# ScalarE issues the mixers' own transfers in a two-layer hybrid backbone block

## The chip, the cores and the metric

The kernel runs on one core of a Trainium2 chip. The metric is the device time in microseconds (us) of one execution. A core has five engines with an instruction stream each: PE (TensorE, matmuls), DVE (VectorE), ACT (ScalarE), POOL (GpSimd) and SP (SyncE, which only issues transfers). Each stream is executed in order: an instruction that waits for a semaphore holds up all that follow it on its engine.

## The reference

Two layers of one trunk work on 512 latent tokens and a prefix of 256 context tokens, 1024 channels each, all in float32:

```
for layer in range(2):
    p_lat, p_ctx = (modulated rmsnorm of x, of ctx) @ w_in          # 1024 -> 256 + 1560 + 1536 columns
    y = concat(s5_mixer, gdn_mixer, rwkv_mixer)                     # three groups of heads
    x = x + gt1 * (y_lat @ w_out)
    x = x + gt2 * (square(relu(h @ w1)) @ w2)                       # h: modulated rmsnorm, 1024 -> 4096 -> 1024
    if layer == 0: the same for ctx with y_ctx
return rmsnorm(x)
```

The S5 mixer is a complex diagonal scan in both directions. The gated DeltaNet (GDN) and RWKV-7 mixers have 6 heads of 64 channels each. Both are delta rules: in chunks of 64 tokens they need the inverse of a unit triangular 64x64 matrix per chunk, head and direction, and then a scan over the chunks, from both ends. The latents' scans start from the state that the context's scans leave.

## The kernel before

Activations lie with channels on the 128 partitions and tokens in the free dimension, 256 for the context and 512 for the latents.

**Dense work.** The projections, the modulations and the MLP stream their weights from DRAM. `weight` (L265) loads a tile of 128x512 into one of four staging tiles `wl` (L271, issued by SP), ACT casts it to the rounded format in one of three `wh` (L272), and POOL or DVE subtracts to get the rest in one of two `wo` (L273). `product` (L290) then runs three matmuls per weight and activation tile (L296) into the PSUM bank `d`. The modulations (`mods`, L921) load float32 weights (L934) and multiply them as they are (L937).

**Mixers.** `run_jobs` goes through 12 pairs of jobs, one GDN and one RWKV job of two heads each: three pairs for each of context and latents in both layers. For a pair come, in this order, `prep` of both jobs, `solve`, `prep2`, `post` of both (after `level2`, which joins the inverses of 32x32 blocks to those of 64x64), `chain` and `readout`. `solve` (L335) brings the blocks through DRAM into a layout with a problem in each partition (L352, L363, L364), inverts them on DVE (L368 to L373) and takes them back (L376 to L386), all with transfers issued by SP. ACT copies a half of the matrices in it (L366, L375).

A job moves its own data by these lines, all of which SP issues before the change:
- `source` (L1319) loads a projection that `front` stored to DRAM (L1028): keys, queries, values, decays and gates, in `prep` and `readout`.
- `park` (L1326) stores a tile to a DRAM scratch until it is wanted: GDN's queries and attention matrices, RWKV's bonus, its read matrices `R` and its transposed `kb`.
- `fetch` (L1332) loads a parked tile back in `post` or `readout`.
- In `GdnJob.post`, L1469 loads halves of the parked attention matrices beside the scaled queries, which ACT copies in L1470.

Of the code that reads or writes what they carry: ACT's L1562 squares a key that `source` loaded; POOL's L1465 scales the queries that `fetch` loaded; ACT's L1656 evicts what `prep2` parks; PE's L481 transposes.

**Memory and order.** Tiles of the mixers and activations are pieces of 18 pages in SBUF (`s`, L184). A piece that is taken again waits until its last readers are done. The order of the instructions on each engine is written when the kernel is built, by the scheduler of the tile framework: it takes the instructions with priorities (`prio`, L117; classes L33, chains first, dense work late), runs them through its own estimate of times, and puts each into the stream of its engine when its operands are there by that estimate. The hooks of `run` (L1252) say behind which pair the dense stages are traced.

Of the kernel before, what the change touches and what calls it, by code (L numbers as in the profile page):

```python
# [89 lines left out]
class Kern:  # L90
# [132 lines left out]
    def wide(self, tag, dt=F32):  # L223
        return self.wp.tile([P, 512], dt, tag=tag, name=self.nm(tag), bufs={"wl": 4, "wh": 3, "wo": 2}[tag])
# [259 lines left out]
    def by_head(self, p, nt, flip, keep):  # L484

        nc = self.nc
        o = self.s(nt * 128, keep=keep).rearrange("p (c v) -> p c v", v=64)
        for h in range(2):
            for r, rs in enumerate(HALVES):
                nc.scalar.copy(o[HALVES[1 - h if flip else h], r::2], p[rs].rearrange("p (t h v) -> p t h v", t=nt, h=2)[:, :, h])  # L490
        return o
# [814 lines left out]
class Job:  # L1306
# [9 lines left out]
    def source(self, j, keep=None):  # L1316
        K = self.K
        t = K.s(self.part.n, keep=keep)
        K.nc.sync.dma_start(t, K.pd[self.l, self.part][j])  # L1319
        return t  # L1320

    def park(self, name, t):

        w = t.shape[-1]
        dram = self.K.scratch(f"{name}{w}", [P, w], 3)
        self.K.nc.sync.dma_start(dram, t)  # L1326
        return dram

    def fetch(self, dram, keep):
        w = dram.shape[-1]  # L1330
        t = self.K.s(w, keep=keep)
        self.K.nc.sync.dma_start(t, dram)  # L1332
        return t

    def gather(self, ot, po, n):
# [11 lines left out]
class GdnJob(Job):  # L1347
# [82 lines left out]
    def post(self):  # L1430

        K, f, part, nt = self.K, self.f, self.part, self.nt
        nc, gd, n, C = K.nc, K.gd[self.l, part], part.n, part.nc
        K.level2(lambda h: nt, self.ytt, C, "q")
        wide = lambda keep: K.s(128 * C, keep=keep).rearrange("p (n d v) -> p n d v", d=2, v=64)
        ne = wide(None)
        nc.vector.tensor_tensor(ne, nt, gd["neg"][:, :, f].rearrange("p d c -> p c d").unsqueeze(3).to_broadcast([P, C, 2, 64]), OP.mult)
        self.W, self.TV = wide(self.till_chain), wide(self.till_chain)
        for n0 in range(0, C, 4):
            for w in range(2):  # L1440
                ps = K.ps("q").rearrange("p (n d v) -> p n d v", d=2, v=64)
                for i in range(4):
                    for d in range(1 if w else 2):
                        c = part.chunk(d, n0 + i)
                        for h, hs in enumerate(HALVES):
                            if w:
                                nc.tensor.matmul(ps[HALVES[1 - h], i], self.ku[hs, c], ne[hs, c], start=True, stop=True)
                            else:
                                nc.tensor.matmul(ps[hs, i, d], nt[hs, c, d], self.vh[hs, c], start=True, stop=True)
                nc.scalar.copy((self.W if w else self.TV)[:, n0:n0 + 4], ps)  # L1450


        self.kh, self.out = [], []
        for d in range(2):
            x = K.s(n, keep=self.till_chain).rearrange("p (c k) -> p c k", c=C)
            nc.gpsimd.tensor_tensor(x, self.ku, gd["bk"][:, d, f].unsqueeze(2).to_broadcast([P, C, 64]), OP.mult)
            self.kh.append(x)
        if self.emit:
            q_tm = self.fetch(self.q_tm, None)
        for d in range(2 if self.emit else 0):  # L1460
            x = K.s(2 * n, keep=self.till_chain).rearrange("p (h t) -> p h t", h=2)
            with K.scope():
                qd = K.s(n)
                by_head = lambda z: z.rearrange("p (t h k) -> p t h k", t=part.nt, h=2)
                nc.gpsimd.tensor_tensor(by_head(qd)[:, :, ::-1], by_head(q_tm),  # L1465
                                        gd["eg"][:, d, :, 2 * f:2 * f + 2].unsqueeze(3).to_broadcast([P, part.nt, 2, 64]), OP.mult)
                ps = K.transposed(qd, part.nt, "q")
                for h, hs in enumerate(HALVES):
                    nc.sync.dma_start(x[hs, h], self.at[hs, d * n:(d + 1) * n])  # L1469
                    nc.scalar.copy(x[HALVES[1 - h], h], ps[HALVES[1 - h]])  # L1470
            self.out.append(x)
        K.release(self.till_post)
# [68 lines left out]
class RwkvJob(Job):  # L1541
# [121 lines left out]
    def post(self):  # L1663
# [6 lines left out]
        for n0 in range(0, part.nc, 4):  # L1670
            with K.scope():
# [19 lines left out]
                for h, hs in enumerate(HALVES):  # L1691
                    nc.scalar.copy(xv[h][hs, nn], ps[hs])
        fetch = lambda t, p: self.fetch(t, self.till_chain).rearrange(p, i=64, n=part.nc)
        self.kb = [fetch(t, "p (n h i) -> p n h i") for t in self.kb]
        self.R = [fetch(t, "p (h n i) -> p h n i") for t in self.R]
        K.release(self.till_post)

# [230 lines left out]
```

## Time and profile before

| | |
|---|---|
| median of 3 runs | 3006.74 us (2999.44 to 3011.88) |
| profiled execution | 2999.21 us, of which the span of the trace is 2997.4 us |
| granted TensorE clock, mean | 0.883 of full speed |
| busy: PE, DVE, ACT, POOL | 2656.7, 1583.8, 1204.1, 1049.6 us |
| transfers | 401.65 MB, the 16 DMA engines 42.9% busy with those of the program |

The page gives busy times, the span in slices, the costliest groups of instructions and the issues of transfers. Engines are named as above, PEld is the loading of weights into PE, SPq is SP's stream. A row such as `ACT wh L272 <- PE d L296: 406.1, 238, 6.7` says that ACT, before the instructions of line 272 that write `wh`, waited 406.1 us in total, 238 times, 6.7 us at the longest, and that the wait ended when PE finished an instruction of line 296. In the timelines the bracket at a row's end gives the engine's idle time before the instruction and what ended it; "issue" means that the profile shows nothing that did. Issuing a transfer does not count as busy time.

### The profile page before, as it was taken

The numbers are of one execution on the slowest core, as the hardware profiler recorded it, in microseconds if no ns is written. First come the engines' busy times: TensorE is split into PE (matmuls) and PEld (weight loads), VectorE is DVE, ScalarE is ACT, GpSimd is POOL, SyncE is SP. The second block draws the span as 40 slices with busy tenths as digits, with TensorE's granted clock in tenths as the row PEclk, the third lists the DMA queues.
The fourth block names the chain that finished last, engine by engine and source line by source line (L and its number), as shares of the span: only waits on it lengthen the run. The fifth ranks groups of instructions, "written<-read, shape, count | busy, mean of one in ns | idle before, by whom it ended". The sixth has DMA issues, their size and how long they took to land. (4 is left out here: it accounts for less than half of the span.)

```text
span 2997.4 us, 54389 instructions
## 1 busy us (share of the span) xinstructions
PE 2656.7 (89%) x20052; PEld 2042.6 (68%) x20052; DVE 1583.8 (53%) x4047; ACT 1204.1 (40%) x2460; POOL 1049.6 (35%) x1227
## 2 busy tenths in 40 slices
PE   5889998876899999987989989889888989799998
PEld 2767875654668888866667777667655566478776
DVE  7744874764557756557765531547656353321213
ACT  3344443232435444455433434454333332243333
POOL 1432333423132221222447434343433323144443
PEclk9889997676899999977999999889987868699999
DMA  5445545544764544443343332365465622023222
GB/s 208 107 146 174 154 127 178 154 138 123 219 176 153 153 156 129 153 130 122 89 107 130 107 90 93 106 199 161 140 210 183 195 79 84 28 92 95 93 95 85
DMA packets 324650, 401.65 MB, mean 134 GB/s; under 512 B 142880, under 2 KB 173472, under 8 KB 324384
## 3 DMA queue, kind: packets, MB, share of 16 engines
q1 hardware_dynamic: 324384, 398.18, 42.9%
q8 instruction: 158, 2.59, 0.4%
q14 instruction: 108, 0.88, 0.1%
HBM read 300.70 MB, written 88.90 MB: 130 GB/s over the span
## 5 line engine op out<-in xcount | busy, mean ns | idle before, releaser
L296 PE MATMUL d<-page,wh 128*128 128x512 f32 (+1 forms) x5024 | 1416.2, 366 | 61.7 <-DVE page L1164 23.2
L296 PEld LDWEIGHTS d<-page,wh 128*128 128x128 f32 x5024 | 920.3, 196 | 229.7 <-DVE page L1164 27.2
L296 PE MATMUL d<-page,wo 128*128 128x512 f32 (+1 forms) x2512 | 919.5, 366 | 12.3 <-POOL wo L273 7.3
L273 POOL TENSOR_TENSOR wo<-wl,wh 128x512 fp32r<-128x512 f32 (+1 forms) x357 | 477.9, 1339 | 719.3 <-PE d L296 555.7
L272 ACT CAST wh<-wl 128x512 fp32r<-128x512 f32 (+1 forms) x590 | 360.2, 616 | 585.6 <-PE d L296 406.1
L296 PEld LDWEIGHTS d<-page,wo 128*128 128x128 f32 x2512 | 494.0, 197 | 90.4 <-POOL wo L273 10.8
L273 DVE TENSOR_TENSOR wo<-wl,wh 128x512 fp32r<-128x512 f32 (+1 forms) x233 | 167.1, 718 | 133.0 <-PE d L296 54.0
L285 DVE TENSOR_TENSOR page<-s,page 128x512 fp32r<-128x512 f32 (+1 forms) x118 | 76.3, 647 | 275.5 <-ACT page L284 271.5
L1164 DVE SCALAR_TENSOR_TENSOR page<-d,mod,page 128x512 f32<-128x512 f32 (+1 forms) x192 | 124.8, 658 | 166.9 <-PE d L296 166.1
L371 DVE TENSOR_TENSOR solve<-solve 128x30 f32<-128x30 f32 (+4 forms) x360 | 149.8, 416 | 44.5 <-issue 23.2
L373 DVE TENSOR_TENSOR solve<-solve 128x30 f32<-128x30 f32 (+4 forms) x360 | 138.3, 384 | 8.0
L1507 POOL TENSOR_TENSOR g<-g,gates 64x128 f32<-64x128 f32 x120 | 55.1, 459 | 228.6 <-DVE g L1512 209.0
L937 PE MATMUL d<-wl,sc 128*32 128x512 f32 x320 | 109.6, 723 | 8.2 <-DMA wl<-in_mod_w_dram 6.7
L1154 ACT ACTIVATE s<-d 128x512 f32<-128x512 f32 (+1 forms) x96 | 50.6, 527 | 148.4 <-PE d L296 148.2
L472 DVE SCALAR_TENSOR_TENSOR s<-s,ncol,s 128x256 f32<-128x256 f32 (+1 forms) x132 | 92.7, 707 | 17.7 <-ACT s L470 13.3
L481 PE MATMUL p<-consts,page 128*128 128x128 f32 x348 | 64.1, 310 | 32.9 <-ACT page L1656 10.0
L1630 PEld LDWEIGHTS p<-page,page 64*128 64x128 f32 x576 | 73.9, 211 | 21.2 <-issue 12.9
L1630 PE MATMUL p<-page,page 64*128 64x128 f32 (+1 forms) x576 | 85.9, 310 | 0.0
L1741 PE MATMUL rc<-page,page 128*64 128x64 f32 x464 | 84.1, 268 | 1.7 <-DMA page<-dr 1.7
L1740 PE MATMUL rc<-page,r 64*64 64x64 f32 x432 | 77.5, 265 | 8.8 <-DVE r L1732 3.6
L481 PEld LDWEIGHTS p<-consts,page 128*128 128x128 f32 x348 | 42.3, 154 | 55.6 <-ACT page L1656 12.3
L1718 DVE TENSOR_TENSOR page<-page,rc 64x128 f32<-64x128 f32 x144 | 40.8, 284 | 66.1 <-PE rc L1716 50.3
(459 smaller groups left out, 3916.0 us busy)
## 6 DMA issues: line engine op xcount, KB each, us to landing
wl<-in_w_dram SPq DMA_DIRECT2D x384, 256.0 KB, 2.7
wl<-in_mod_w_dram SPq DMA_DIRECT2D x160, 256.0 KB, 3.6
wl<-in_w_in_dram SPq DMA_DIRECT2D x142, 256.0 KB, 2.9
page<-dr SPq DMA_DIRECT2D x118, 256.0 KB, 3.4
dr<-s SPq DMA_DIRECT2D x72, 256.0 KB, 2.8
dr<-page SPq DMA_DIRECT2D x30, 512.0 KB, 4.5
dr<-page SPq DMA_DIRECT2D x55, 256.0 KB, 2.9
page<-dr SPq DMA_DIRECT2D x16, 834.0 KB, 5.0
```

The costliest lines, as they stand in the source:

```text
L272: nc.scalar.copy(hi, st)
L273: low.tensor_tensor(lo, st, hi.bitcast(F32), OP.subtract)
L296: nc.tensor.matmul(ps, x, y, start=(first and i == 0), stop=(last and i == len(order) - 1))
L371: nc.vector.tensor_tensor(tm, y3[:, :j, j:j + 1].to_broadcast([P, j, w]), y3[:, j:j + 1, j + 1:].to_broadcast([P, j, w]), OP.mult)
L373: nc.vector.tensor_tensor(y3[:, :j, j + 1:], y3[:, :j, j + 1:], tm, OP.add)
L472: nc.vector.scalar_tensor_tensor(acc, cp[:, j:j + n], w[:, 5 * i + j:5 * i + j + 1], acc, OP.mult, OP.add)
L481: self.nc.tensor.transpose(p[:, t * 128:(t + 1) * 128], src[:, t * 128:(t + 1) * 128], self.ident)
L937: nc.tensor.matmul(ps[32 * i:32 * i + 32], self.sc[:, k0 + i], t, start=(k0 == 0), stop=(k0 == 4))
L1164: nc.vector.scalar_tensor_tensor(x[j], ps, mod[:, 40 + j, g:g + 1], x[j], OP.mult, OP.add)
L1630: nc.tensor.matmul(ps[:, i], flat(bk[d][hs, n0 + i]), kr[d][hs, n0 + i], start=True, stop=True)
L1740: nc.tensor.matmul(o, st[hs, d], kr[d][hs, n, 1], start=True, stop=False)
L1741: nc.tensor.matmul(o, xv[h][:, n, d], self.R[d][:, h, n], start=False, stop=True)
```

## The change

In four places a transfer is issued by ACT (`nc.scalar.dma_start`) and not by SP (`nc.sync.dma_start`). Sources, destinations and sizes are the same. Loads of weights, the stores of `front`, the transfers of `solve`, those of the S5 mixer and of the readout to `w_out` stay with SP.

```diff
     def source(self, j, keep=None):
         t = K.s(self.part.n, keep=keep)
-        K.nc.sync.dma_start(t, K.pd[self.l, self.part][j])
+        K.nc.scalar.dma_start(t, K.pd[self.l, self.part][j])
         return t
     def park(self, name, t):
         dram = self.K.scratch(f"{name}{w}", [P, w], 3)
-        self.K.nc.sync.dma_start(dram, t)
+        self.K.nc.scalar.dma_start(dram, t)
         return dram
     def fetch(self, dram, keep):
         t = self.K.s(w, keep=keep)
-        self.K.nc.sync.dma_start(t, dram)
+        self.K.nc.scalar.dma_start(t, dram)
         return t
...
                 for h, hs in enumerate(HALVES):
-                    nc.sync.dma_start(x[hs, h], self.at[hs, d * n:(d + 1) * n])
+                    nc.scalar.dma_start(x[hs, h], self.at[hs, d * n:(d + 1) * n])
                     nc.scalar.copy(x[HALVES[1 - h], h], ps[HALVES[1 - h]])
```

## Rows read from the trace of the kernel before

**Rows 1.** Page, section 1: busy us, share of the span, instructions
```profile
PE 2656.7 (89%) x20052; PEld 2042.6 (68%) x20052; DVE 1583.8 (53%) x4047; ACT 1204.1 (40%) x2460; POOL 1049.6 (35%) x1227
```

**Rows 2.** Stretches: length, busy us of PE, PEld, DVE, ACT, POOL, clock, DMA share
```profile
700.00:800.00 100.00, 74.40 (x606) 43.57 (x607) 43.06 (x123) 32.52 (x62) 29.81 (x30) 0.79 0.61 186
1000.00:1100.00 100.00, 99.42 (x1368) 84.41 (x1366) 57.31 (x148) 47.29 (x104) 23.50 (x36) 1.00 0.55 166
```

**Rows 3.** Waits of PE: engine, tile, line, releaser: total us, times, longest
```profile
PE p L481 <- ACT page L1656: 10.0, 3, 7.4
PE p L330 <- ACT page L1562: 9.4, 5, 3.5
PE q L481 <- POOL page L1465: 8.7, 3, 4.6
PE p L481 <- DMA page<-dr: 6.7, 6, 2.6
PE gc L1519 <- DMA page<-dr: 2.1, 3, 1.5
PE rc L1741 <- DMA page<-dr: 1.7, 1, 1.7
PE gc L323 <- ACT page L321: 0.2, 1, 0.2
```

**Rows 4.** Waits of all engines, same columns
```profile
ACT wh L272 <- PE d L296: 406.1, 238, 6.7
POOL page L1465 <- DMA page<-dr: 97.5, 6, 37.8
ACT page L1562 <- DMA page<-dr: 20.1, 4, 8.7
```

**Rows 5.** Lines L1319, L1326, L1332, L1469: issue ns min/median/max, first and last start
```profile
L1319 SPq DMA_DIRECT2D page<-dr x132: 314/376/842, 172.1 to 2501.1; - x132
L1326 SPq DMA_DIRECT2D dr<-page x69: 319/338/1267, 205.0 to 2398.1; - x69
L1332 SPq DMA_DIRECT2D page<-dr x60: 319/376/1573, 358.9 to 2513.0; - x60
L1469 SPq DMA_DIRECT2D page<-dr x36: 444/468/810, 215.6 to 2486.5; - x36
```

**Rows 6.** Waits of SP, which issues the transfers: total us, times, longest
```profile
SPq L271 <- POOL wo L273: 796.7, 273, 69.0
SPq L1319 <- DMA dr<-s: 26.9, 21, 3.2
SPq L1326 <- ACT page L1656: 14.6, 12, 5.7
SPq L1319 <- DMA wl<-in_w_dram: 0.5, 1, 0.5
```

**Rows 7.** Timelines of SP and ACT from 424: start, us, instruction [idle before]
```profile
431.89 0.40 SPq L1319 DMA_DIRECT2D page<-dr  x1
432.34 2.98 SPq L386 DMA_DIRECT2D page<-dr  x6
435.43 1.31 SPq L1319 DMA_DIRECT2D page<-dr  x3
439.25 0.51 ACT L1562 ACTIVATE page<-page,cols 128x256 f32<-128x256 f32 x1 [8.75 <-DMA page<-dr]
```

**Rows 8.** Timelines of ACT and PE from 612, same columns
```profile
622.50 1.92 ACT L366 COPY solve<-solve 64x1024 f32<-64x1024 f32 x1 [6.80 <-issue]
625.08 1.11 PE L481 MATMUL p<-consts,page 128*128 128x128 f32 x4 [7.44 <-ACT page L1656]
```

**Rows 9.** SP's timeline from 12; issues (KB, us to landing); SP's waits
```profile
14.16 23.02 SPq L934 DMA_DIRECT2D page<-in_mod_w_dram  x32
page<-in_mod_w_dram SPq DMA_DIRECT2D x32, 256.0 KB, 5.4
SPq L934 <- DMA page<-in_mod_w_dram: 9.0, 24, 1.3
```

## The prediction

> **What bounds the kernel now.** I read the page's busy times first [rows 1]: PE is busy 2656.7 of 2997.4 us, ACT 1204.1 (40%). PE sets the time, so an edit is worth only what it takes from or adds to PE's 340 us of idle time, or to its clock. The stages [rows 2] are unlike: between 1000 and 1100 PE is busy 99 us in 100 at full clock. Nothing is to be gained there, and delays are absorbed by weight tiles cast ahead. Between 700 and 800 PE is busy 74 us in 100 at a granted clock of 0.79, and ACT only 32.5: there the mixers' latency sets the pace, and dense work is too thin to fill the holes.
>
> PE's own waits [rows 3] tell who releases it. The view has 92 rows, 329.2 us in 248 waits; 36 rows name ACT, 99.0 us in 82 waits (the first and last of these stand there). Transfers that the change moves release PE in 10.5 us (6.7 + 2.1 + 1.7). The longest waits of other engines for them lead to two more PE waits: 9.4 us behind ACT's L1562 and 8.7 behind POOL's L1465 [rows 3, 4].
>
> **What moves.** Four lines issue the moved transfers [rows 5]: 132 + 69 + 60 + 36 = 297. At the medians they take 132 x 0.376 + 69 x 0.338 + 60 x 0.376 + 36 x 0.468 = 112.4 us of SP's time. This leaves SP and goes to ACT's instruction stream. Bytes, sizes and number of transfers stay; so does the arithmetic. The order on each engine is written anew at build time, so the placement of each issue is not known from the trace; I give that 15 us either way, half the sum of the gains below, as an estimate.
>
> **Taken from SP: 0 by itself.** SP waits 796.7 us before weight loads for the subtraction that frees a staging tile [rows 6]. Its time isn't scarce; only transfers stuck behind others count.
>
> **Transfers that come sooner: between 0 and -28.6 us, I take -9.5.** The upper gain is all PE waits above: 10.5 + 9.4 + 8.7 = 28.6. What speaks for it is one burst [rows 7]: SP issues one L1319, six transfers of the inverses and three L1319 without a pause, and ACT sits idle 8.75 us before L1562 until an L1319 lands. Issued by the idle ACT, the three would not stand behind the six (2.98 us). Against it: the flight of each transfer stays, and POOL's 97.5 us for L1465 [rows 4] lead to only 8.7 on PE. A third seems nearest to what the queue alone causes. It cannot be below nothing by itself; the harm is counted next.
>
> **Issues on ACT: between 0 and +112.4 us of PE time, I take +9.2.** No row shows a DMA issued by ACT, so I use SP's durations. At the low end every issue falls in ACT's 1793 us of idle time; at the high end each delays PE by its full length. Between them I go by the row nearest: PE waits 99.0 us for 1204.1 us of ACT's work, 0.082 us each. 112.4 x 0.082 = 9.2.
>
> **Waits on ACT: between 0 and +209 us, I take +17.2.** A transfer waits at the head of its engine's stream. Before the four lines SP waited 243.2 us in 155 waits (64 rows; the first and the last stand there, [rows 6]), 33.9 of them for ACT itself, as 14.6 for L1656. Those vanish when ACT issues after its own write; 209.3 stay: landing of the projections (26.9), tiles not yet released, results of DVE. On SP they cost nothing but prefetch. On ACT, what is queued behind are casts of weights (L272), evictions of PSUM and copies of the mixers, and PE waits for these. What that means is shown by one wait that ACT has now [rows 8]: between 615.7 and 622.5 it stood 6.80 us before L366 (the view names no releaser; the copy reads what L364 loads); L1656 was queued behind, and PE then idled 7.44 us for L1656. That is one for one. But ACT also waits 406.1 us for PE before L272 in the dense stages [rows 4], where it runs ahead and a wait is free. I take the ratio above: 209.3 x 0.082 = 17.2. One for one only in the 40% of time in which ACT has work would make (112.4 + 209.3) x 0.40 = 129 us, an upper end for both together. What is late next is the staging of weights: ACT's cast frees nothing until it runs, then SP's load waits too.
>
> **Sum.** -9.5 + 9.2 + 17.2 = +16.9 us. On the profiled execution's 2999.21 us (span 2997.4 and 1.8 around it) that is 3016.1; that execution lies 7.5 below the median of the runs, 3006.74, and so I forecast 3006.74 + 16.9 = 3023.6, say 3024 us. One half per cent, 15 us, is about what a measurement of this kernel can tell from no change. The forecast lies just beyond it.
>
> **A rule of the skill.** Every transfer of the trace is issued by SP, so what two issuers gain is not shown. The Trainium skill, "DMA: Bandwidth & Descriptors", section "Issuing engines are not separate DMA queues", says that transfers started by different engines share the same 16 DMA engines, and that starting them from several saves only the sequencer's issue time. By that rule the gain would be part of 112.4 us of an engine that isn't short of time: 0, not -9.5, and the sum +26.4.
>
> **Rivals.**
> *Faster: the mixers' chain gets shorter.* In the stretches like 700 to 800 [rows 2] PE waits for the mixers, and ACT is idle two thirds of the time. If ACT's waits there fall in idle time, the full 28.6 us come back, and the clock with less idle time rises from 0.79; nothing is paid. For it: the burst of rows 7, and SP stuck before L271 for up to 69 us [rows 6] with mixers' transfers behind. Against it: few of those waits reach PE. About 3007 - 29 = 2978 us. It decides if the issues land where ACT would have waited for a mixers' transfer anyway.
>
> *No change.* The transfers are hidden both ways: only 10.5 us of PE's 329 are theirs now, and ACT's 60% idle time takes 112 us of issue. Waits that SP had came from its running ahead of the others; ACT reaches the same transfer later, when it is ready. Then 3007 us, give or take 10.
>
> *Much slower: the transfers hold each other.* A load seems to wait for an older load that has nothing to do with it [rows 9]: 32 loads into separate tiles go out in 23.02 us, 0.72 us apart, and take 5.4 us to land; 5.4 / 0.72 = 7.5 in flight, and 24 of SP's waits in that line are for the landing of another such load. So about eight are let out at a time, in rotation (an estimate from these rows). If ACT's transfers take their turns in the same rotation, SP's weight load waits until ACT has come to a mixers' transfer, and ACT waits for loads of weights that SP holds back. Price: 297 turns at 0.2 us, a quarter of the 0.82 us (243.2 / 297) that a moved transfer waited on average, is 59 us: 3007 + 59 = 3066 us. It decides when ACT stands before transfers for longer than the four staged weight tiles last.
>
> That the change does nothing of what it says I hold impossible: it names the issuing engine on the four lines. That the new order puts the issues elsewhere in the stream than today is in the 15 us.
>
> **Chances and range.** Forecast (3009 to 3039, its own range): 0.38. Faster chain: 0.28. No change: 0.22. Rotation: 0.12. Beyond half a per cent slower lie 0.25 of the forecast's chance, the rotation's 0.12 and 0.01 of no change: 0.38. Within it: 0.13 of the forecast, 0.18 of no change, 0.03 of the faster: 0.34. Faster: 0.25 and 0.03 of no change: 0.28. For the range I go from 2978 less 10 of the 15 for the order, 2968, to the rotation's 3066. The 129 us of the upper end (3136) stay outside, as does what the order might do beyond 15 us.
>
> **What would show it.** Right: 297 issues on ACT's sequencer with about 0.4 us each; waits of ACT's sequencer before L1319, L1326, L1332 and L1469; PE's waits for ACT above 99 us, by some 25; PE's waits for moved transfers, L1562 and L1465 below 28.6; PE's busy share lower between 500 and 800 and in 2000 to 2500; SP's waits for weights shorter where ACT is late with L272. Rotation: waits of SP's weight loads for the landing of the mixers' transfers. The forecast is wrong if PE's waits for ACT stay at 99 us, or if 500 to 800 gets shorter by more than 15 us. If PE's waits are as now in total and the time still differs, the clock or the order did it, and not the steps above.

## The result and the profile after

The changed kernel takes 3034.56 us (median of 4 runs, 3031.37 to 3035.84); the kernel before took 3005.21 us in the same comparison (4 runs, 2999.44 to 3011.88). The ratio is 1.0102, 95% interval [1.0083, 1.0121]: 1% slower, 29.35 us between the medians and 30.7 by the ratio. The forecast was 3024.

The page of the changed kernel, busy times [rows 1] and queues of transfers; a queue's row gives packets, MB and the share of 16 engines' span:

```profile
span 3034.1 us, 54363 instructions
...
PE 2687.9 (89%) x20052; PEld 2059.4 (68%) x20052; DVE 1596.3 (53%) x4047; ACT 1202.5 (40%) x2460; POOL 1058.0 (35%) x1227
...
q1 hardware_dynamic: 283920, 321.09, 35.1%
q10 hardware_dynamic: 40464, 77.09, 7.8%
```

The span grew by 36.7 us (2997.4 to 3034.1). PE runs the same 20052 matmuls but is busy 31.2 us longer; its idle time grew by 5.5 us only (340.7 to 346.2). So the time went into longer matmuls: the mean granted clock fell from 0.883 to 0.873. Read alone, PE's 89% on both pages would say that nothing happened. The Trainium skill, "Perfetto Trace Analysis", section "Identifying the Most-Contended Engine", says that matmul busy time is no good measure of how near TensorE is to its best; the 31.2 us more for equal work agree, though by the clock and not by the overlap of matmuls, which is the reason that the page gives.

The moved transfers now go out on ACT's stream, on a queue of their own, q10. The issues of the four lines [rows 5], duration in ns, then first and last start:

```profile
L1319 ACTq DMA_DIRECT2D page<-dr x132: 320/327/1433, 170.1 to 2540.0; - x132
L1326 ACTq DMA_DIRECT2D dr<-page x69: 323/327/462, 203.6 to 2437.4; - x69
L1332 ACTq DMA_DIRECT2D page<-dr x60: 321/327/1928, 360.9 to 2550.0; - x60
L1469 ACTq DMA_DIRECT2D page<-dr x36: 451/463/1598, 215.0 to 2524.7; - x36
```

At the medians that is 261 x 0.327 + 36 x 0.463 = 102.0 us of ACT's stream; with the long ones it sums to 117.2. Waits of its stream ahead of the four lines, added up from its semaphore instructions, come to some 200 to 215 us, by where a wait is taken to begin.

PE's waits, those of [rows 3] and the longest new ones: total us, times, longest.

```profile
PE d L937 <- DMA wl<-in_mod_w_dram: 20.5, 11, 4.0
PE d L821 <- DMA page<-dr: 16.4, 6, 4.8
PE p L481 <- DMA page<-dr: 15.6, 9, 7.1
PE q L1447 <- ACT page L1450: 8.8, 1, 8.8
PE p L330 <- ACT page L1562: 5.1, 3, 3.8
PE q L481 <- POOL page L1465: 1.6, 3, 0.7
PE gc L1519 <- DMA page<-dr: 1.5, 2, 0.8
PE p L481 <- ACT page L1656: 0.4, 1, 0.4
```

The rows for ACT sum to 85.3 us (35 rows, 78 waits), less than the 99.0 of before; all rows sum to 335.4 (329.2). An ACT that stands 200 us before transfers does not hold PE up more often. This is the case that the forecast named last: PE's waits nearly as before, and the time differs.

Where it differs shows when the two traces are laid side by side by the k-th run of a line. At 624, 927, 1196, 1871 and 2062 us of the kernel before, the changed kernel is late by -11, +9, +12, 0 and -1 us; at 2403 us it is at +36, and it stays at +37 to the end. In these two traces all of the net loss arises between 2062 and 2403 us, in the last three pairs, the latents of the second layer. The stretches there, before and then after (length, busy us of PE, PEld, DVE, ACT, POOL, clock, DMA share, GB/s):

```profile
2300.00:2400.00 100.00, 90.74 (x799) 53.70 (x801) 41.61 (x103) 34.11 (x65) 44.56 (x44) 0.87 0.63 197
2400.00:2500.00 100.00, 89.18 (x1247) 69.56 (x1239) 50.59 (x151) 33.83 (x71) 25.39 (x36) 0.73 0.33 101
```

```profile
2300.00:2400.00 100.00, 88.00 (x630) 48.51 (x632) 35.04 (x91) 22.64 (x48) 34.94 (x40) 0.67 0.54 165
2400.00:2500.00 100.00, 85.57 (x1058) 67.41 (x1056) 47.54 (x144) 29.73 (x60) 20.29 (x31) 0.59 0.32 88
```

One place seems to say why. ACT's timeline of the changed kernel, from 2222 us:

```profile
2225.03 1.17 ACT L1640 COPY page<-p 64x512 f32<-64x512 f32 x2
2238.18 0.35 ACTq L1326 DMA_DIRECT2D dr<-page  x1
2240.59 0.24 ACT L857 COPY page<-d 128x96 f32<-128x96 f32 x1 [14.39 <-PE d L856]
2243.28 0.62 ACT L1641 COPY page<-page 64x512 f32<-64x512 f32 x1 [2.45 <-PE p L1638]
2243.92 0.58 ACT L1640 COPY page<-p 64x512 f32<-64x512 f32 x1
2243.93 0.35 ACTq L1319 DMA_DIRECT2D page<-dr  x1
```

The same two copies in the trace of before:

```profile
2234.26 0.61 ACT L1641 COPY page<-page 64x512 f32<-64x512 f32 x1 [7.04 <-PE p L1638]
2246.19 0.24 ACT L857 COPY page<-d 128x96 f32<-128x96 f32 x1 [1.60 <-PE d L856]
```

ACT stands 14.39 us, 9.5 of them at a store (L1326) whose semaphore was still held by a store of the blocks to be inverted (L352), which SP had issued only at 2233.93; the S5 mixer's copy (L857) and the RWKV job's (L1641) are behind it. In the trace of before L1641 comes first and L857 later. Two causes lie in this one picture: the stop, and the order in which L857 stands ahead of L1641. The experiments take them apart.

### The profile page after: what moved, and what is told of

Same layout as the page of the kernel before. It is cut to its first block, busy times and chain, and to the rows that moved or that the text cites. A ratio compares the mean times of both kernels' runs of the same rounds, so it can differ in the third digit from the quotient of the medians.

```text
span 3034.1 us, 54363 instructions
## 1 busy us (share of the span) xinstructions
PE 2687.9 (89%) x20052; PEld 2059.4 (68%) x20052; DVE 1596.3 (53%) x4047; ACT 1202.5 (40%) x2460; POOL 1058.0 (35%) x1227
## 5 line engine op out<-in xcount | busy, mean ns | idle before, releaser
L272 ACT CAST wh<-wl 128x512 fp32r<-128x512 f32 (+1 forms) x590 | 359.7, 615 | 528.4 <-PE d L296 410.8
L937 PE MATMUL d<-wl,sc 128*32 128x512 f32 x320 | 116.4, 761 | 23.0 <-DMA wl<-in_mod_w_dram 20.5
L1630 PE MATMUL p<-page,page 64*128 64x128 f32 (+1 forms) x576 | 91.6, 324 | 0.9 <-ACT page L1640 0.9
L1630 PEld LDWEIGHTS p<-page,page 64*128 64x128 f32 x576 | 78.3, 223 | 20.5 <-issue 10.8
L1741 PE MATMUL rc<-page,page 128*64 128x64 f32 x464 | 88.3, 280 | 0.0
L481 PE MATMUL p<-consts,page 128*128 128x128 f32 x348 | 62.4, 305 | 19.3 <-DMA page<-dr 15.6
L1727 POOL TENSOR_TENSOR r<-r,wc 128x128 f32<-128x128 f32 x54 | 25.7, 476 | 131.9 <-DVE r L1732 104.3
```

The costliest lines, as they stand in the source:

```text
L272: nc.scalar.copy(hi, st)
L937: nc.tensor.matmul(ps[32 * i:32 * i + 32], self.sc[:, k0 + i], t, start=(k0 == 0), stop=(k0 == 4))
L1630: nc.tensor.matmul(ps[:, i], flat(bk[d][hs, n0 + i]), kr[d][hs, n0 + i], start=True, stop=True)
L1741: nc.tensor.matmul(o, xv[h][:, n, d], self.R[d][:, h, n], start=False, stop=True)
```

## The experiments

Three theories. **A**: ACT stands in order before transfers that aren't ready, and delays what is behind. **B**: the issues take ACT's time. **C**: the planner (the scheduler that writes the order when the kernel is built), which writes the order on every engine anew when a transfer changes its engine, wrote a worse one. The forecast is A and B with an allowance for C. Ratios are to the kernel before in the same comparison.

**One line at a time, and one stage.** In the first three kernels only the named lines have the new issuer; in the fourth all four lines, for the last three pairs alone:

```diff
+        self.q = K.nc.scalar if l == 1 and part is LAT else K.nc.sync
...
-        K.nc.sync.dma_start(t, K.pd[self.l, self.part][j])
+        self.q.dma_start(t, K.pd[self.l, self.part][j])
```

> Only the 132 loads of projections go to ACT. Before: 3005 us; all four lines on ACT: 3035 us (+29). Theory A (ACT stands in order before transfers that are not ready, and what is queued behind is late for PE): ACT waited 77 of 215 us before this line, so about +10, 3015 us, with ACT's waits before the line near 77 us. Theory B (the issue itself costs ACT time): 132 of 297 issues, +13, 3018 us. Theory C (the new order of instructions, not the engine): no relation to the count; anything from -15 to +15 and the three parts do not add up to +29.

> Only the 69 stores of parked tiles go to ACT. Theory A: ACT waited 74 us before this line with all four moved, the longest of them 9.5 us with PE idle for 8.8 us right behind: +10 to +15, 3015 to 3020 us, and a PE wait for ACT's L1450 or L1656 of some us behind such a store. Theory B: 69 of 297 issues, +7, 3012 us. Theory C: from -15 to +15, no relation to the count.

> Only the 96 loads of parked tiles (L1332, L1469) go to ACT. Theory A: ACT waited 64 of 215 us before these lines: +8, 3013 us. Theory B: 96 of 297 issues, +9, 3014 us. Theory C: from -15 to +15.

> All four lines go to ACT, but only in the last three pairs of jobs (latents of layer 1, 87 of the 297 transfers). In the changed kernel the last three pairs' work runs 0 us late at 1871 us and 36 us late at 2440 us, and stays so. Theory A (waits of ACT in a stage that the mixers' latency paces): the whole loss is here, +25 to +40, 3030 to 3045 us. Theory B (issue cost, spread evenly): 87 of 297, +9, 3014 us. Theory C: the order ahead of these pairs is as before, what follows may fall either way: -15 to +15.

| moved | transfers | us | ratio | ACT stood before them, one trace |
|---|---|---|---|---|
| L1319 | 132 | 3028.04 | 1.0078 [1.0055, 1.0102] | 61.7 us |
| L1326 | 69 | 3003.47 | 0.9997 [0.9978, 1.0015] | 59.6 us |
| L1332, L1469 | 96 | 3011.48 | 1.0018 [1.0001, 1.0036] | 55.9 us |
| all, last three pairs | 87 | 3023.85 | 1.0056 [1.0034, 1.0077] | 87.2 us |

ACT stands nearly as long in each of the first three, and the losses are 23, -1 and 7 us. They add up to the whole 29 us, which the expectation for C had ruled out. But the first lies beyond all three expectations and the second meets C's alone: neither standing nor the number of issues goes with the loss, and A and B in that form are in trouble. The order of every engine is new in each of these kernels, so they don't separate the theories. The fourth, between A's 3030 and B's 3014, has 0.56 of the 1.02% with 87 transfers in the last three pairs.

**Issuer and order taken apart.** The order of a program can be given to another: behind the building of the kernel each instruction is tied to the one that stood before it on its engine, with an edge that orders and adds no wait.

```diff
+        hold_order(tc)
...
+            if last is not None:
+                tc.add_manual_dep(built[k], last.name,
+                                  mb.DependencyInfo(mb.DependencyClass.NoSync, mb.DependencyReason.DATA), reason="order")
+            last = built[k]
```

`ORDER` lists the places of one program's plan. The 297 transfers are left free, so that the planner finds them a place; all else stands as in the other program. The traces bear it out: with the order of before held, POOL's 1227 and ACT's 2460 instructions run in just the sequence of before. No kernel was run that is tied to its own order, so what holding costs by itself is not shown; it is counted with the issuer below. A third kernel is a control: one idle load of 128x2 words at the start, no order held.

> All four lines are issued by ScalarE as in the changed kernel, but every engine is held to the order of the kernel before: TensorE, VectorE, GpSimd, ScalarE's computing instructions and SyncE's remaining transfers stand in the very order that the planner made when SyncE issued everything; only the 297 moved transfers find their places among ScalarE's instructions anew. Theory A+B (issuing on ScalarE itself costs: it stands before transfers that aren't ready and spends 117 us on issuing): the loss stays, 3022 to 3038 us. Theory C (the planner, which lays out all engines anew when the issuer changes, made a worse order): the loss goes, 3000 to 3010 us, and if the earlier start of the transfers is worth something, below 3000.

> The opposite corner: SyncE issues every transfer as before, but TensorE, VectorE, GpSimd, ScalarE's computing instructions and SyncE's other transfers are held to the order that the planner made for the changed kernel. Theory A+B: with nothing issued on ScalarE the loss is gone, 3002 to 3010 us. Theory C: the order brings the loss with it, 3025 to 3040 us.

> The kernel before with one more transfer at its start: SyncE loads 128x2 words of the constants into a tile that nothing reads. It costs at most one issue (about 0.4 us by the issue rows) and takes work from no engine, but the planner lays out all engines anew: 6 to 19% of each engine's instructions change places. Theories A and B: within 3 us of the kernel before. Theory C, with orders scattering by what a change of issuer moved: off by 5 to 25 us either way.

| | order of before | order of the changed kernel |
|---|---|---|
| SP issues | 1 | 1.0085 [1.0054, 1.0115] |
| ACT issues | 1.0026 [1.0004, 1.0049] | 1.0102 [1.0083, 1.0121] |

The control took 0.9995 [0.9972, 1.0017]. The order alone costs 0.85%, some 25 us, with SP issuing as ever; the new issuer alone costs 0.26%, some 8 us (1 to 15). Their sum, 1.11%, is the loss within the intervals. C holds for the larger part, A and B for the smaller. The control says that not every new order costs: 6 to 19% of each engine's instructions moved for nothing, where C had expected 5 to 25 us either way.

The stop in the timeline above turns out to belong to the order as well. In the order of the changed kernel with SP issuing, no store stands on ACT, and ACT idles as long at the same place:

```profile
2234.56 0.24 ACT L857 COPY page<-d 128x96 f32<-128x96 f32 x1 [14.33 <-PE d L856]
2237.25 0.62 ACT L1641 COPY page<-page 64x512 f32<-64x512 f32 x1 [2.45 <-PE p L1638]
```

L857 waits for PE's L856 in both; the 9.5 us at the store lay within that wait.

With ACT issuing in the order of before, PE's waits show the issuer's own price, total us, times, longest:

```profile
PE p L481 <- ACT page L1656: 10.1, 3, 7.7
PE p L481 <- DMA page<-dr: 8.0, 7, 2.2
PE q L481 <- POOL page L1465: 7.2, 4, 4.5
PE p L330 <- ACT page L1562: 5.5, 3, 3.0
PE rc L1741 <- DMA page<-dr: 2.4, 1, 2.4
PE gc L1519 <- DMA page<-dr: 1.2, 2, 0.6
```

The five rows that the forecast hoped to gain (28.6 us, [rows 3]) are 8.0 + 7.2 + 5.5 + 2.4 + 1.2 = 24.3: 4.3 gained. PE's waits for ACT without L1562's rose from 89.6 to 101.3 (106.8 in all): 11.7 lost. Net +7.4, and the measured ratio is worth 7.8. These are one trace each: over all rows PE's waits rose from 329.2 to 339.8. PE's busy time is 2655.2, as before (2656.7).

**Which part of the order.** The lag in the trace of the run with the changed kernel's order, SP issuing, is -7 at 2225 us, +25 at 2394. So the next kernels change order at about 2215 us, and most of the 297 transfers are held with it: one takes the order of before up to there and the changed kernel's behind it, SP issuing; one the reverse, ACT issuing. The trace of the run with only L1326 moved ran 12 to 15 us ahead of before until 2240 us and lost that by 2310. The last two take its order up to 2215 us and that of before behind it; L1326 is ACT's in the first nine pairs in the one, and SP issues all in the other.

```diff
-        self.K.nc.sync.dma_start(dram, t)
+        (self.K.nc.sync if self.l == 1 and self.part is LAT else self.K.nc.scalar).dma_start(dram, t)
```

> SyncE issues every transfer, and every engine keeps the order of the kernel before up to about 2215 us; from there on the order is the changed kernel's (TensorE 473 of 14311 instructions, VectorE 252 of 4049, ScalarE 45, GpSimd 30 stand elsewhere than before). Theory T (the loss is made by the planner's order of the last pairs' preparations alone): 3018 to 3030 us against about 3000. Theory W (the whole order is a little worse everywhere, and the stretch after 2215 us only shows it): under 3010 us.

> The changed kernel, ScalarE issuing all 297 transfers, with its own order up to about 2215 us and the order of the kernel before from there on. Theory T: the loss shrinks to what issuing costs on ScalarE, 3000 to 3012 us against about 3000 (the kernel with the whole order of before measured 1.0026 of before). Theory W: most of the loss stays, 3018 to 3034 us. Issuing on ScalarE as the cause: 3025 to 3034 us.

> Only the parking stores (L1326) on ScalarE, and only in the first nine pairs; the order is that of the kernel with the parking stores moved up to about 2215 us, and from there on that of the kernel before. In the trace of the kernel with the parking stores moved the milestones ran 12 to 15 us ahead of before until 2240 us and lost that until 2310 us. Theory T: the lead is kept, 2983 to 2993 us against about 3000. Theory W, or a lead that only one execution had: within 5 us of before.

> The same order as in the run with the parking stores of the first nine pairs on ScalarE, but SyncE issues everything. If the lead comes from the order: the same 2983 to 2993 us. If it comes from the stores being issued by ScalarE: back to before, 2997 to 3005 us.

| order up to 2215 us, then | issuer of the four lines | us (before: 3005.11) | ratio |
|---|---|---|---|
| before, then changed | SP | 3037.47 | 1.0099 [1.0060, 1.0137] |
| changed, then before | ACT | 3010.84 | 1.0020 [0.9992, 1.0048] |
| L1326-moved, then before | L1326 by ACT in nine pairs | 2988.46 | 0.9947 [0.9929, 0.9964] |
| L1326-moved, then before | SP | 2991.06 | 0.9957 [0.9943, 0.9972] |

The order behind 2215 us makes the loss by itself, as theory T has it: 473 of PE's 14311 instructions, 252 of DVE's, 45 of ACT's and 30 of POOL's stand elsewhere, and no issuer has changed. Give the changed kernel the old order there, and it is within 0.5% of before. The first expectation's upper end, 3030, was passed by 7 us, and the interval covers it. The six executions of that kernel are wide apart, from 3009.65 us at a granted clock of 0.879 to 3048.03 at 0.864: in one and the same order, clock and time go together.

What the loss is made of, in that kernel against before, over the same work (lags of +9 and +47 at its ends); the trace is of an execution of 3043.31 us, so it shows more than the mean loss. Stretches, before and then the one with the changed order behind 2215 us:

```profile
2215.00:2440.00 225.00, 193.04 (x2141) 127.70 (x2140) 120.18 (x364) 79.60 (x160) 67.78 (x85) 0.79 0.58 178
```

```profile
2224.00:2487.00 263.00, 224.08 (x2149) 151.82 (x2152) 123.31 (x363) 78.61 (x158) 67.33 (x85) 0.68 0.50 152
```

The counts agree within a few records. Of the 38 us more, 31 are matmuls that take longer and 7 idle time (31.96 to 38.92); the granted clock fell from 0.79 to 0.68. The clock has two levels, 1.2 and 2.4 GHz; a mean of 0.79 is 42% of the time at the lower one, 0.68 is 64%.

The whole order of the one kernel with the issuer of the other, over the same work: first the changed kernel's order with SP issuing, then the order of before with ACT issuing.

```profile
2208.00:2466.00 258.00, 216.91 (x2152) 144.88 (x2148) 122.10 (x357) 78.74 (x158) 67.86 (x85) 0.70 0.50 154
```

```profile
2220.00:2449.00 229.00, 192.48 (x2160) 127.32 (x2160) 120.45 (x366) 79.73 (x160) 68.57 (x85) 0.81 0.57 177
```

In this stretch the clock and the time go with the order and not with the issuer. In the first, 24 of the 33 us more are matmuls and 9 idle time. Over its whole span it is 10.4 us of busy time (2667.1) and 12.9 of idle time more than before, with a clock a little higher elsewhere (0.81 for 0.80 between 500 and 1000 us); the share of idle time holds for the stretch alone.

The matmuls of L1630 show the clock: ns min, median and max in the stretch, before and then that kernel.

```profile
L1630 PE MATMUL p<-page,page x128: 272/272/374, 2215.3 to 2388.2; 64*128 64x128 f32 x128
```

```profile
L1630 PE MATMUL p<-page,page x125: 272/417/580, 2223.8 to 2435.1; 64*128 64x128 f32 x125
```

In the order, one step of the last RWKV job stands out, DVE's scan over the decays (L1576), once for each direction: duration, then the first and the last start, before and then that kernel.

```profile
L1576 DVE TENSOR_TENSOR_SCAN page<-consts,page x2: 1226/1292/1358, 2309.8 to 2344.5; 128x512 f32<-128x512 f32 x2
```

```profile
L1576 DVE TENSOR_TENSOR_SCAN page<-consts,page x2: 1224/1224/1225, 2317.9 to 2382.2; 128x512 f32<-128x512 f32 x2
```

The second direction's scan comes 34.7 us after the first in the one order, 64.3 in the other. Between them now stands an L1588 of the first direction, which before comes behind both. The job falls back against the dense work: its L1630, at 2367 us in the trace of before, is 51 us late, the L937 at 2354 only 25. That this step makes the loss is read from the traces and not tested: holding one engine's order alone wasn't tried, since the engines' orders wait for each other. Why the planner's estimate chose this order is open.

The last two kernels kept the lead of the order up to 2215 us and are 0.5% and 0.4% faster than before. With SP issuing everything the gain is there too, so it is the order's; the intervals overlap, and no gain of the issuer can be told from them.

**The issuer's price once more**, in the best order: ACT issues all 297, the order is that of the last kernel above.

> All 297 transfers on ScalarE, as in the changed kernel, but TensorE, VectorE, GpSimd and ScalarE's computing instructions in the faster order of the run in which SyncE issued everything (0.9957 of before). If the price of issuing on ScalarE adds to whatever order stands (it was 1.0026 with the order of before): 0.998 to 0.999 of before. If this order was good only because of who issues: 1.005 or more. If the moved transfers' earlier start is worth something in it: 0.994 or less.

It took 3001.53 us, before 3003.19: 1.0001 [0.9976, 1.0026]. Against the same order with SP issuing, 0.9957 in another comparison, that is about +0.44%, with an uncertainty near 0.3; the first measure, 0.26%, lies within it. Both kernels of this pair are held, so holding is no part of this price. It was expected at 0.998 to 0.999, which the interval covers. PE's waits for ACT go from 86.6 to 91.5 us between these two traces, all its waits from 310.9 to 328.8. Issuing from ACT costs an estimated 8 to 13 us, with intervals that reach down to 1 and to 4 us, and the earlier start of the transfers does not pay for it.

## Why the prediction was right in its sign and short of the whole

**Where it failed: the order.** "The order on each engine is written anew at build time ... I give that 15 us either way". This term stood in the range at nothing on the mean. It measured +25 us (0.85% [0.54, 1.15]), beyond the 15, and is the largest of all. It wasn't to be read from the trace of before; but the plan of the changed kernel can be laid beside the old one before anything runs, and there the L1588 between the two L1576 can be seen. What it costs only a run could tell.

**Issues and waits on ACT: right in kind, under half in size.** The forecast took 9.2 + 17.2 = 26.4 us, at 0.082 us of PE for each of ACT's. In the order of before ACT stood 185.6 us before the moved lines (209 estimated) and PE waited 11.7 us longer for ACT: with 102 us of issues 0.041 per us. Of the waits 109.5 us were for results of compute, 40.2 for other transfers and 34.6 for older transfers of SP. The ratio over all of ACT's work was too dear. Part of the reason is in the traces: an issue can run while ACT still executes the instruction before it, as L1319's at 2243.93 us above lies within L1640's; of the 111 us of issues in the run with the order of before, 45 lie so. That the waits fall where ACT has slack behind it, as before L272 [rows 4], is likely and not shown.

**Transfers that come sooner: -4.3 for -9.5.** Mostly L1562 (9.4 to 5.5). What the forecast set against its gain held: the flight stays, 3.6 us at the median for ACT's loads of 256 KB and 3.4 before. By the rule of the Trainium skill that it weighed ("DMA: Bandwidth & Descriptors", "Issuing engines are not separate DMA queues": only issue time is saved) nothing was to be gained; the 4.3 us of one trace lie near that.

**The sum** of these, +16.9, is +7.4 in the order of before, by PE's waits. That 3024 comes within 11 us of 3034.56 is luck: two terms too large and one left out.

**The signs that it asked for.** 297 issues on ACT: yes. ACT's waits before the lines: yes. PE's waits for ACT above 99 by some 25: no, 85.3, because the new order has fewer of them (79.0 with SP issuing); in the old order 106.8, a rise of 8. The forecast called itself wrong if these waits stay at 99 us: by that, its steps did not make the changed kernel's time. Gain rows below 28.6: yes, 23.8 (15.6 + 5.1 + 1.6 + 1.5, and no row for L1741). SP's waits for weights shorter: no, before L271 SP waits 834.5 + 309.0 us for POOL and DVE, 796.7 + 272.0 before. PE's busy share between 500 and 800: higher, 243.07 for 234.36 us of 300; between 2000 and 2500: lower, 434.30 for 441.68 of 500, at a clock of 0.78 for 0.84.

**The rivals.** *Faster*: the shorter chain did not come; the clock fell. *No change*: right for the issuer in the old order, +0.26%. *Rotation*: it is there. In this program each transfer takes the next of eight semaphores, whichever engine issues it, and waits for the older one on it. In the changed kernel ACT stood 39 us for SP's (9 waits, 9.5 the longest, in the timeline above), and SP 12 us for ACT's (11 waits). But the price of 59 us is refuted: all that the issuer costs is some 8 to 13.

## What to carry to other kernels

Where a planner writes the order, an edit to one line changes the program everywhere: hold the order and change the issuer, then hold the issuer and change the order, before a loss is put down to the line that was edited. A timeline that shows a stop at the edited line (14.39 us here) proves little: in the same order with the old issuer the stop is there without the line (14.33 us). And an order is worth a search of its own: the best here is 0.5% faster than the kernel before, and 0.4% comes with no change of issuer.

## What the hardware showed

In the stretch of the loss a worse order cost little idle time on TensorE, 7 of 38 us in one trace and 9 of 33 in another. The rest came with a lower granted clock, 0.68 and 0.70 for 0.79, with L1630's median at 417 ns for 272. Whether work in more broken pieces lowers the clock, or another cause lowers it with the order, the runs don't separate.

An issue takes 0.33 us of ACT's instruction stream (0.46 for L1469's), somewhat less than the 0.34 to 0.47 on SP [rows 5], and part of it runs beside ACT's computing. In this program the transfers of both engines share one rotation of eight semaphores.
